# Matmuls of 274 columns, two of them shared between neighbours, in place of 272

## The chip, the core and the metric

The program runs on one core of one Trainium2 chip. TensorE (PE in the profile) multiplies, with its weight loads shown apart as PEld; VectorE (DVE), ScalarE (ACT) and GpSimd (POOL) work element by element, and SyncE (SP) issues most DMAs. The metric is the device time of one execution in microseconds. Three runs of the kernel before took 2904.58, 2910.63 and 2912.99 us, a median of 2910.63 us. The profile comes from one more execution, of 2907.33 us.

## The reference

One inference step of a decoder trunk of two layers, model width 1024, over 1024 new prompt tokens and 64 sample tokens (8 sequences of 8), in float32:

```python
# layer 0: short gated convolution, layer 1: differential attention
gb, gc, h = jnp.split(x @ w_in, 3, axis=-1)            # w_in: 1024 x 3072
...                                                    # u = gc * h, three taps over time
y = (gb * conv) @ w_out
xp = _layernorm(ALPHA * xp + mp, ln_mix_g[i], ln_mix_b[i])

def _swiglu(x, w_in, w_out):                           # w_in: 1024 x 5632, w_out: 2816 x 1024
    gate, up = jnp.split(x @ w_in, 2, axis=-1)
    return (jax.nn.silu(gate) * up) @ w_out
xp = _layernorm(ALPHA * xp + _swiglu(xp, w_ffn_in[i], w_ffn_out[i]), ln_ffn_g[i], ln_ffn_b[i])
```

The three products that matter here are `x @ w_in` of the convolution and of the two feed-forward blocks. Attention, with its cache of 2048 past positions for each sample sequence, lies between them and is not touched.

## The kernel before

**The input products.** Each of the three large products is done by a Strassen scheme with seven smaller products in place of eight. Tokens are cut into two halves of 544 columns (`HALF`), and inputs and outputs into halves of their features. For the inputs, seven combinations of the four blocks lie in SBUF, each split into a high and a low part of the type float32r (`Combos`, tiles `xh` and `xl`, of 128 partitions, 7 operands, 4 blocks of 128 features and 544 columns). Weights are combined and split in the same way on the way in (`Weights.make`: tiles `ws`, made by a copy on ACT, L76, and a subtraction on DVE, L77).

**One product.** `in_type` (L216) runs a list of work items. An item is seven products, numbered 1 to 7, in an order written out in `order`; a product is done by `mm` (L233). Since a bank of PSUM holds 512 float32 values and a half has 544 columns, `mm` takes the half in two chunks of `CW` = 272 columns, one in each of two banks. For each chunk it runs over 4 blocks of 128 features and over 3 passes (high times high, high times low, low times high): 12 matmuls for a chunk, 24 for a product, each with its own weight load and a moving operand of 128 partitions by 272 columns (L240). Convolution has 12 items, each feed-forward block 22, so there are 56 x 7 x 24 = 9408 such matmuls.

**What follows a product.** Products 1, 6, 5 and 3 of an item add up in one pair of banks (tile `pin1`), 7 and 4 in another, 2 in a third. After 1, 6 and 5 ACT copies the sum so far out of PSUM (L254); after 2, 5 and 4 DVE adds a sum to a copy (L258); after 3 the item's class ends it (`put.last`). Both read the two chunks in one instruction, as 2 runs of 272 columns.

**What sets the order.** On PE the order inside `in_type` is that of the code (`manual_schedule`). On ACT, DVE, POOL and SP a scheduler of the framework places the instructions; it estimates when each can start. Weights are made up to seven products ahead (`prep`).

**The other stages.** Output products (`out_type`, L321) use matmuls of 512 columns with three passes; the projections of attention (L930) use matmuls of 256 columns with the same three passes, between which single steps of the sample attention run.

Of the kernel before, what the change touches and what calls it, by code (L numbers as in the profile page):

```python
# [14 lines left out]
ALU = mybir.AluOpType  # L15
# [11 lines left out]
CH = ((0, 32), (32, 32), (64, 240), (304, 272), (576, 240), (816, 272))  # L27
HALF = NT // 2
CW = HALF // 2
TT = (0,) + tuple(NS + P * i for i in range(NP // P))  # L30
F = 2816
FT = F // P
# [16 lines left out]
def decoder_kernel(ctx: ExitStack, tc: tile.TileContext, i_: dict, o_: dict):  # L49
    nc = tc.nc  # L50
    PE, ACT, DVE, POOL, SP = nc.tensor, nc.scalar, nc.vector, nc.gpsimd, nc.sync
# [36 lines left out]
    def passes(ah, al, bh, bl):  # L88
        return ((ah, bh), (ah, bl), (al, bh))
# [126 lines left out]
    def in_type(psum, x, work):  # L216


        order = [(0, 1), (0, 2)]
        for n in range(len(work)):  # L220
            order += [(n, 7), (n, 6)] + ([(n + 1, 1)] if n + 1 < len(work) else []) + [(n, 5)]
            order += ([(n + 1, 2)] if n + 1 < len(work) else []) + [(n, 4), (n, 3)]
        made, nxt = {}, 0
        banks = {}

        def prep(upto):
            nonlocal nxt
            while nxt < min(upto, len(order)):
                n, p = order[nxt]
                made[n, p] = work[n][0].make(p)  # L230
                nxt += 1

        def mm(ps, w, p, start, chunks=(0, 1)):  # L233
            for c in chunks:
                cs = slice(c * CW, c * CW + CW)
                for k in range(4):
                    ks = slice(k * P, k * P + P)
                    b = OPERAND[p]
                    for m, (a, y) in enumerate(passes(w[:, 0, ks], w[:, 1, ks], x.h[:, b, k, cs], x.l[:, b, k, cs])):
                        PE.matmul(ps[:, c, :CW], a, y, start=(start and k == 0 and m == 0),  # L240
                                  stop=(k == 3 and m == 2), skip_group_check=True)

        prep(6)
        with tc.manual_schedule(engines={mybir.EngineType.PE}):
            for at, (n, p) in enumerate(order):
                put = work[n][1]
                w = made.pop((n, p))
                if p in (1, 2, 7):
                    banks[n, p] = psum.tile([P, 2, 512], F32, name=f"pin{p}", tag="b")
                ps = banks[n, {1: 1, 6: 1, 5: 1, 3: 1, 7: 7, 4: 7, 2: 2}[p]]  # L250
                mm(ps, w, p, p in (1, 2, 7))
                v = ps[:, :, :CW]
                if p in (1, 6, 5):
                    ACT.copy(put.dst({1: 0, 6: 2, 5: 3}[p]), v)  # L254
                if p in (2, 5, 4):
                    blk = {2: 0, 5: 3, 4: 2}[p]
                    d = put.dst(blk)
                    DVE.tensor_tensor(d, d, banks[n, 7][:, :, :CW] if p == 5 else v, op=ALU.add)  # L258
                    put.done(blk)
                elif p == 3:  # L260
                    put.last(v)
                prep(at + 7)
# [171 lines left out]
    def ffn_in(layer, psum, xc):  # L434
        with tc.tile_pool(name=f"fst{layer}", bufs=2, reuse_waits="tile") as stage:
            class Put:
                def __init__(self, f):
                    self.f, self.sg, self.hf = f, {}, None

                def gate(self, t):  # L440
                    if t not in self.sg:
                        self.sg[t] = stage.tile([P, 2, CW], F32, name=f"sg{t}", tag=f"sg{t}", bufs=2 - t)
                    return self.sg[t]

                def dst(self, blk):
                    if blk == 0:
                        return self.gate(0)
                    if self.hf is None:
                        self.hf = stage.tile([P, 2, 2, CW], F32, name="hf", tag="hf")
                    return self.hf[:, blk - 2]  # L450

                def done(self, blk):
                    if blk == 0:
                        ACT.activation(self.sg[0], self.sg[0], AF.Silu)
                    elif blk == 2:
                        DVE.tensor_tensor(self.hf[:, 0], self.hf[:, 0], self.sg[0], op=ALU.mult)

                def last(self, ps):
                    ACT.activation(self.gate(1), ps, AF.Silu)
                    DVE.tensor_tensor(self.hf[:, 1], self.hf[:, 1], self.sg[1], op=ALU.mult)  # L460
                    SP.dma_start(h_dram[layer][self.f], self.hf.rearrange("p a c n -> p (a c n)"))

            in_type(psum, xc, [(Weights(i_["wfi"][layer, 2 * f], i_["wfi"][layer, 2 * f + 1]), Put(f))
                               for f in range(FT)])
# [9 lines left out]
    with tc.tile_pool(name="psum0", bufs=4, space=PSUM) as psum:  # L474
        with tc.tile_pool(name="xc0", bufs=1, reuse_waits="tile") as xcp:
            xc = Combos(xcp)

            with tc.tile_pool(name="cvp", bufs=1, reuse_waits="tile") as cvp:
# [11 lines left out]
                for ch in range(2):  # L490
                    blk = {}
                    for t, k in ((0, 0), (0, 1), (1, 0), (1, 1)):
                        x = blk[k, t] = cv("u" if t else "gc")[:, 0:4 * CW].rearrange("p (k t) -> p k t", k=4)
                        at = 0
# [4 lines left out]
                    cs = slice(ch * CW, ch * CW + CW)  # L499
# [110 lines left out]
                for f0 in range(0, KT, 2):  # L610
                    gate = Gate(f0)
                    for m, put in ((1, gate), (2, Mix(f0, gate)), (0, Out(f0, gate))):
                        work.append((Weights(i_["wci"][3 * f0 + m], i_["wci"][3 * f0 + 3 + m]), put))
                in_type(psum, xc, work)
                POOL.dma_start(o_["conv_p"], cpT)
                POOL.dma_start(o_["conv_s"], csT)
# [16 lines left out]
    with tc.tile_pool(name="kvp", bufs=1, reuse_waits="tile") as kvp, \  # L633
# [276 lines left out]
        with tc.manual_schedule(engines={mybir.EngineType.PE}):  # L910
            for pr in range(4):
                for ty, dst in enumerate((q_dram, o_["k_p"], o_["v_p"])):
# [6 lines left out]
                    for tg in range(2):  # L919
                        nat = ap2.tile([P, 4, 256], F32, name="nat", tag="pr", bufs=4)  # L920
                        first = pr == ty == tg == 0
                        ps = [None] * 4
                        for kh, t in [(kh, t) for kh in range(2) for t in range(4)] if first else [(None, t) for t in range(4)]:
                            t0 = TT[1 + 4 * tg + t]
                            if t % 2 == 0 and not kh:
                                ps[t] = ps[t + 1] = ps2.tile([P, 2, 512], F32, name="psqkv", tag="s2")
                            for k in range(KT) if kh is None else range(4 * kh, 4 * kh + 4):
                                cs = slice((k % 4) * 256, (k % 4) * 256 + 256)
                                for n, (a, b_) in enumerate(passes(xTh, xTl, his[k // 4], los[k // 4])):
                                    PE.matmul(ps[t][:, t % 2, :256], a[:, k, t0:t0 + P], b_[:, cs],  # L930
                                              start=(k == 0 and n == 0), stop=(k == KT - 1 and n == 2),
# [85 lines left out]
        def mixed(h, i, r1, A, vn, ost):  # L1017
            aT = ap2.tile([P, KT, P], F32, name="aT", tag="aT", bufs=1)
            for g4 in range(0, i + 1, 4):
                m = min(4, i + 1 - g4)  # L1020
                ps = psb.tile([P, 4, P], F32, name="psaT", tag="pb")
                for k in range(m):
                    PE.transpose(ps[:, k, :], A[:, (g4 + k) * P:(g4 + k + 1) * P], ident)  # L1023
                (ACT.copy if g4 == 0 else DVE.tensor_copy)(aT[:, g4:g4 + m, :], ps[:, :m, :])
            return h, i, r1, aT, vn, ost
# [34 lines left out]
        for h in range(NH):  # L1060
# [4 lines left out]
            for n in range(8):  # L1065
# [4 lines left out]
                m = mixed(*todo.pop(0)) if len(todo) == 2 else None  # L1070
# [7 lines left out]
        for x in todo:  # L1078
            m = mixed(*x)
# [115 lines left out]
```

## Time and profile before

| | before |
|---|---|
| runs (us) | 2904.58, 2910.63, 2912.99 |
| profiled execution (us) | 2907.33, its span 2905.6 |
| mean granted TensorE clock | 0.971 |
| PE busy | 2728.5 us, 94% |
| DVE, ACT, POOL busy | 52%, 36%, 9% |
| DMA | 157 GB/s mean |

A matmul's record is longer than the distance to the next one, since matmuls are pipelined and their ends are modelled. The time that a stream of matmuls takes is therefore read from the starts of rows, not from their lengths. Where a row says x2, it stands for two matmuls after one another.

### The profile page before, as it was taken

How to read it: one execution, taken by the hardware profiler on the slowest of the kernel's cores; microseconds unless marked ns; L12 is line 12 of the kernel's file. 1: busy time of each engine (PE TensorE's matmuls, PEld its weight loads, DVE VectorE, ACT ScalarE, POOL GpSimd, SP SyncE). 2: the span in 40 equal slices, each digit the busy share in tenths (PEclk: the TensorE clock that was granted, in tenths of full speed). 3: DMA queues.
4: the chain of work that ended last, by engine and by line, in shares of the span. 5: the costliest groups of instructions: out<-in, count | busy, mean ns of one | idle time of the engine just before them, and what ended most of it. 6: DMA issues, size and time to landing. Idle time of an engine off the chain costs nothing.

```text
span 2905.6 us, 51121 instructions
## 1 busy us (share of the span) xinstructions
PE 2728.5 (94%) x20436; PEld 2364.7 (81%) x20436; DVE 1497.9 (52%) x2565; ACT 1043.0 (36%) x1921; POOL 253.4 (9%) x481
## 2 busy tenths in 40 slices
PE   6999879999998999899999999997889999989997
PEld 6999559999997677689888666665679999986676
DVE  7666476555552365522222666673775555532555
ACT  4222254333332244412122556562543333322343
POOL 0000010000000010111111232330100000000100
PEclk9999989999999999899999999998999999999999
DMA  3111652222223466775877888834622222234666
GB/s 123 67 60 62 199 182 81 75 82 72 79 73 118 139 212 202 228 260 200 278 275 254 287 299 309 288 110 144 211 77 80 73 82 75 75 100 147 203 190 191
DMA packets 187728, 454.95 MB, mean 157 GB/s; under 512 B 36545, under 2 KB 85330, under 8 KB 187490
## 3 DMA queue, kind: packets, MB, share of 16 engines
q1 hardware_dynamic: 175442, 408.88, 42.3%
q0 software_dynamic: 11904, 42.55, 4.3%
q8 instruction: 160, 2.62, 0.4%
q14 instruction: 78, 0.64, 0.1%
q10 hardware_dynamic: 144, 0.26, 0.0%
HBM read 387.44 MB, written 64.17 MB: 155 GB/s over the span
## 4 chain that ended last, share of the span: by engine, by line
PE 64%; issue 23%; DMA 5%; DVE 3%; ACT 2%; POOL 2%; SPq 1%; DVEq 0%; POOLq 0%; ACTq 0%
PE pin L240 25%; PE pout L321 14%; PE psqkv L930 10%; PE psS L995 3%; PE psO L833 3%; PE pso L1030 2%; PE psS L775 2%; PE psaT L1023 1%; PE pouts L324 1%; DMA raw<-wfo 1%; PE psq L717 1%; DMA hr<-h_dram 1%; DVE wlo L77 1%; PE psS L998 1%; DVE xl L77 0%
## 5 line engine op out<-in xcount | busy, mean ns | idle before, releaser
L240 PE MATMUL pin<-xh,ws 128*128 128x272 f32 x6272 | 1199.4, 290 | 39.6 <-ACT ws L76 18.6
L240 PEld LDWEIGHTS pin<-xh,ws 128*128 128x128 f32 x6272 | 1000.3, 190 | 43.4 <-ACT ws L76 19.1
L240 PE MATMUL pin<-xl,ws 128*128 128x272 f32 x3136 | 914.2, 292 | 2.2 <-DVE xl L77 2.1
L240 PEld LDWEIGHTS pin<-xl,ws 128*128 128x128 f32 x3136 | 594.6, 190 | 3.1 <-DVE xl L77 3.1
L321 PE MATMUL pout<-whi,hh 128*128 128x512 f32 x960 | 391.4, 409 | 56.6 <-ACT hh L76 43.6
L77 DVE TENSOR_TENSOR wlo<-raw,whi 128x1024 fp32r<-128x1024 f32 x204 | 250.8, 1230 | 291.0 <-ACT whi L76 260.7
L321 PE MATMUL pout<-whi,hl 128*128 128x512 f32 x960 | 381.5, 400 | 4.2 <-DVE hl L77 4.2
L321 PE MATMUL pout<-wlo,hh 128*128 128x512 f32 x960 | 381.2, 398 | 0.0
L76 ACT CAST whi<-raw 128x1024 fp32r<-128x1024 f32 x204 | 213.6, 1048 | 287.7 <-DMA raw<-wfo 145.6
L321 PEld LDWEIGHTS pout<-whi,hh 128*128 128x128 f32 x960 | 184.3, 192 | 145.9 <-ACT hh L76 69.2
L77 DVE TENSOR_TENSOR ws<-s,ws 128x512 fp32r<-128x512 f32 x224 | 154.5, 690 | 141.6 <-ACT ws L76 141.0
L930 PE MATMUL psqkv<-whi,xTh 128*128 128x256 f32 x768 | 222.6, 290 | 2.4 <-DVE xTl L77 2.4
L321 PEld LDWEIGHTS pout<-whi,hl 128*128 128x128 f32 x960 | 183.9, 192 | 49.5 <-DVE hl L77 8.0
L321 PEld LDWEIGHTS pout<-wlo,hh 128*128 128x128 f32 x960 | 184.5, 192 | 38.2 <-DVE wlo L77 0.3
L930 PE MATMUL psqkv<-wlo,xTh 128*128 128x256 f32 x768 | 214.7, 279 | 0.0
L930 PE MATMUL psqkv<-whi,xTl 128*128 128x256 f32 x768 | 214.4, 279 | 0.0
L76 ACT CAST ws<-s 128x512 fp32r<-128x512 f32 x224 | 138.8, 620 | 205.8 <-PE pin L240 103.8
L77 DVE TENSOR_TENSOR hl<-hr,hh 128x384 fp32r<-128x384 f32 (+1 forms) x180 | 94.4, 525 | 184.0 <-ACT hh L76 183.8
L76 ACT CAST hh<-hr 128x384 fp32r<-128x384 f32 (+1 forms) x180 | 85.4, 475 | 260.8 <-PE pout L321 167.1
L94 POOL TENSOR_SCALAR rs_t<-lss 128x1 f32<-128x1 f32 x32 | 22.0, 686 | 1691.9 <-ACT pout L355 1085.7
L77 DVE TENSOR_TENSOR ws<-raw,ws 128x512 fp32r<-128x512 f32 x168 | 115.4, 688 | 99.6 <-ACT ws L76 99.6
L930 PEld LDWEIGHTS psqkv<-whi,xTh 128*128 128x128 f32 x768 | 145.0, 189 | 18.0 <-issue 14.1
(219 smaller groups left out, 3269.7 us busy)
## 6 DMA issues: line engine op xcount, KB each, us to landing
raw<-wfo SPq DMA_DIRECT2D x132, 512.0 KB, 3.9
kpg<-ck SPq DMA_DIRECT2D x128, 512.0 KB, 5.3
vpg<-cv SPq DMA_DIRECT2D x128, 512.0 KB, 4.9
raw<-wfi SPq DMA_DIRECT2D x88, 512.0 KB, 3.3
h_dram<-hf SPq DMA_DIRECT2D x44, 544.0 KB, 2.7
raw<-wci SPq DMA_DIRECT2D x24, 512.0 KB, 3.3
raw<-wco SPq DMA_DIRECT2D x24, 512.0 KB, 3.8
x_dram<-x SPq DMA_DIRECT2D x24, 512.0 KB, 3.0
```

Of the source, the lines that this page charges most:

```text
L76: ACT.copy(hi, src)
L77: (eng or DVE).tensor_tensor(lo, src, fv(hi), op=ALU.subtract)
L240: PE.matmul(ps[:, c, :CW], a, y, start=(start and k == 0 and m == 0), stop=(k == 3 and m == 2), skip_group_check=True)
L321: PE.matmul(ps[:, hf, :], a, b, start=(f == 0 and m == 0), stop=(f == nf - 1 and m == 2))
L324: PE.matmul(pq[half * NS:half * NS + NS, 0, :], hs, raw[:, half * 512:half * 512 + 512], start=(f == 0), stop=(f == nf - 1), skip_group_ch ...
L717: PE.matmul(psq[half * NS:half * NS + NS, pr * 256:pr * 256 + 256], xsT[:, 4 * kh + k, :], raws[half][:, k, :], start=(kh == 0 and k == 0) ...
L775: PE.matmul(ps[32 * t:32 * t + 32, n, :], qp[:, 2 * t + h2, :], kp[:, 2 * t + h2, :], start=(h2 == 0), stop=(h2 == 1), skip_group_check=True)
L833: PE.matmul(O[32 * t:32 * t + 32, :], PT[:, p, 32 * t:32 * t + 32], vp[:, 2 * t:2 * t + 2, :].rearrange("p h d -> p (h d)"), start=(p == 0 ...
L930: PE.matmul(ps[t][:, t % 2, :256], a[:, k, t0:t0 + P], b_[:, cs], start=(k == 0 and n == 0), stop=(k == KT - 1 and n == 2), skip_group_che ...
L995: PE.matmul(svs[c][:, bk, :], a[cp, i, :], b_[cp, bk * w:bk * w + w], start=(m == 0), stop=(m == 2), skip_group_check=True)
L998: PE.matmul(svs[c][:, nb - 1, w - P:w], idb, cmask, start=False, stop=True, skip_group_check=True)
L1030: PE.matmul(po, aT[:, k, :], vn[:, k, :], start=(k == 0), stop=(k == i))
```

## The change

`mm` takes chunks of 274 columns. The first reads columns 0 to 273 of the half, the second columns 270 to 543, so that both read columns 270 to 273. The first chunk's results are put from column 2 of its bank and the second's from column 0, so that in both banks the 272 columns that belong to the chunk lie at 2 to 273. All readers take them from there.

```diff
+MW = CW + 2
...
             for c in chunks:
-                cs = slice(c * CW, c * CW + CW)
+                cs = slice(c * (CW - 2), c * (CW - 2) + MW)
+                at = 2 - 2 * c
                 for k in range(4):
...
-                        PE.matmul(ps[:, c, :CW], a, y, start=(start and k == 0 and m == 0),
+                        PE.matmul(ps[:, c, at:at + MW], a, y, start=(start and k == 0 and m == 0),
                                   stop=(k == 3 and m == 2), skip_group_check=True)
...
-                v = ps[:, :, :CW]
+                v = ps[:, :, 2:2 + CW]
...
-                    DVE.tensor_tensor(d, d, banks[n, 7][:, :, :CW] if p == 5 else v, op=ALU.add)
+                    DVE.tensor_tensor(d, d, banks[n, 7][:, :, 2:2 + CW] if p == 5 else v, op=ALU.add)
```

On PE no instruction changes its place; waits do. These are the first matmuls of the program's second product (bank pair `pin_303`), in the first stage, before the change and then after it:

```order
L240 MATMUL pin_303<-xh,ws 128x272 [waits Activation_49]
L240 MATMUL pin_303<-xl,ws 128x272
L240 MATMUL pin_303<-xh,ws 128x272 [waits DVE_49]
L240 MATMUL pin_303<-xh,ws 128x272
L240 MATMUL pin_303<-xl,ws 128x272
```

```order
L244 MATMUL pin_303<-xh,ws 128x274 [waits Activation_49]
L244 MATMUL pin_303<-xl,ws 128x274 [waits DVE_49]
L244 MATMUL pin_303<-xh,ws 128x274 [waits DVE_49]
L244 MATMUL pin_303<-xh,ws 128x274
L244 MATMUL pin_303<-xl,ws 128x274
```

The first chunk's matmuls now wait for the second chunk's inputs as well, of which they read two columns; the second chunk, 12 matmuls later, waited for them anyway.

On ACT and on DVE two neighbours change places in four places each: three in the convolution and one at the start of the first feed-forward block. This is the one on ACT in the feed-forward block, before and then after; `sg_4231` is the copy of a product's sum out of PSUM and `ws` a weight tile for a later product:

```order
L76 CAST ws<-s_4199 128x512
L76 CAST ws<-s_4234 128x512
L254 COPY sg_4231<-pin_4206 128x544
L76 CAST ws<-raw 128x512
L76 CAST ws<-s_4233 128x512
```

```order
L79 CAST ws<-s_4199 128x512
L79 CAST ws<-s_4234 128x512
L79 CAST ws<-raw 128x512
L258 COPY sg_4231<-pin_4206 128x544
L79 CAST ws<-s_4233 128x512
```

The copy out of PSUM has moved behind one cast of a weight tile. On POOL and SP nothing moves.

## Rows read from the trace of the kernel before

**Rows 1.** The page: busy time, share of the span and instructions.

```profile
PE 2728.5 (94%) x20436; PEld 2364.7 (81%) x20436; DVE 1497.9 (52%) x2565; ACT 1043.0 (36%) x1921; POOL 253.4 (9%) x481
```

**Rows 2.** The page: the chain that ended last, by line.

```profile
PE pin L240 25%; PE pout L321 14%; PE psqkv L930 10%; PE psS L995 3%; PE psO L833 3%; PE pso L1030 2%; PE psS L775 2%; PE psaT L1023 1%; PE pouts L324 1%; DMA raw<-wfo 1%; PE psq L717 1%; DMA hr<-h_dram 1%; DVE wlo L77 1%; PE psS L998 1%; DVE xl L77 0%
```

**Rows 3.** Stretches of the input products: length, busy time by engine, clock, DMA.

```profile
core 0: us, PE busy (x) PEld busy (x) DVE busy (x) ACT busy (x) POOL busy (x), PEclk, DMA share, GB/s
30.00:60.00 30.00, 26.30 (x193) 26.14 (x194) 26.77 (x43) 11.82 (x20) 0.20 (x2) 0.87 0.21 71
443.00:480.00 37.00, 33.68 (x246) 32.45 (x245) 28.45 (x44) 18.68 (x31) 0.00 (x0) 0.95 0.24 86
480.00:900.00 420.00, 420.00 (x3340) 420.00 (x3339) 212.70 (x314) 140.51 (x238) 0.00 (x0) 1.00 0.22 76
2129.00:2160.00 31.00, 28.49 (x201) 27.31 (x202) 25.66 (x40) 16.57 (x27) 0.00 (x0) 0.93 0.21 70
```

**Rows 4.** The page: groups of matmuls of the input products.

```profile
L240 PE MATMUL pin<-xh,ws 128*128 128x272 f32 x6272 | 1199.4, 290 | 39.6 <-ACT ws L76 18.6
L240 PE MATMUL pin<-xl,ws 128*128 128x272 f32 x3136 | 914.2, 292 | 2.2 <-DVE xl L77 2.1
```

**Rows 5.** Timeline of PE, 272 columns, steady (start, length, what).

```profile
600.05 0.29 PE L240 MATMUL pin<-xl,ws 128*128 128x272 f32 x1
600.17 0.41 PE L240 MATMUL pin<-xh,ws 128*128 128x272 f32 x2
...
602.82 0.41 PE L240 MATMUL pin<-xh,ws 128*128 128x272 f32 x2
603.07 0.29 PE L240 MATMUL pin<-xl,ws 128*128 128x272 f32 x1
```

**Rows 6.** Timeline of PE, 272 columns, early in the first stage.

```profile
33.70 0.82 PE L240 MATMUL pin<-xh,ws 128*128 128x272 f32 x2 [8.54 <-DVE ws L77]
34.33 0.43 PE L240 MATMUL pin<-xl,ws 128*128 128x272 f32 x1
...
37.05 0.43 PE L240 MATMUL pin<-xl,ws 128*128 128x272 f32 x1
```

**Rows 7.** Granted clock of the stretches of rows 5, 6, 8 and 9.

```profile
core 0: us, PE busy (x), PEclk, DMA share, GB/s
34.00:37.00 3.00, 3.00 (x14) 0.50 0.00 0
400.50:402.60 2.10, 2.10 (x11) 1.00 0.02 4
600.00:603.10 3.10, 3.10 (x27) 1.00 0.02 7
1385.00:1386.10 1.10, 1.10 (x12) 1.00 1.06 331
1404.80:1405.80 1.00, 1.00 (x11) 1.00 0.40 152
```

**Rows 8.** Timeline of PE, 256 columns (L930), in two places.

```profile
1385.01 0.28 PE L930 MATMUL psqkv<-whi,xTl 128*128 128x256 f32 x1
...
1386.07 0.28 PE L930 MATMUL psqkv<-whi,xTl 128*128 128x256 f32 x1
...
1404.78 0.28 PE L930 MATMUL psqkv<-whi,xTl 128*128 128x256 f32 x1
...
1405.80 0.28 PE L930 MATMUL psqkv<-whi,xTl 128*128 128x256 f32 x1
```

**Rows 9.** Timeline of PE, 512 columns (L321).

```profile
400.51 0.39 PE L321 MATMUL pout<-whi,hh 128*128 128x512 f32 x1
...
402.57 0.39 PE L321 MATMUL pout<-wlo,hh 128*128 128x512 f32 x1
```

**Rows 10.** Timeline of DVE ahead of the first stage's second product.

```profile
30.56 1.28 DVE L77 TENSOR_TENSOR xl<-u,xh 128x1088 fp32r<-128x1088 f32 x1
31.76 1.28 DVE L507 TENSOR_TENSOR u<-u,gc 128x1088 f32<-128x1088 f32 x1
32.96 0.68 DVE L77 TENSOR_TENSOR ws<-raw,ws 128x512 fp32r<-128x512 f32 x1
```

**Rows 11.** Waits: engine, line, waited for: us in total, times, longest.

```profile
ACT hf L254 <- PE pin L240: 186.4, 88, 4.4
```

## Prediction

> **What bounds the kernel now.** I read the page's busy times first. PE is busy for 94% of the span, DVE for 52%, ACT for 36% [rows 1]. The chain that ended last puts its largest share, 25%, on the line that the change touches [rows 2]. Then I cut the input products into stretches. In the steady one, 480 to 900 us, PE is busy for all of 420 us at a granted clock of 1.00, while DVE works 212.7 us, ACT 140.5 us and the DMA engines 22% [rows 3]. So there the stream of matmuls alone sets the time, and what one matmul costs there is paid 1:1. In the first microseconds of each of the three input stages it is otherwise: DVE works 26.8 of 30, 28.5 of 37 and 25.7 of 31 us, PE has gaps, and the three stretches hold 193 + 246 + 201 = 640 matmuls [rows 3]. There are 6272 + 3136 = 9408 matmuls of this line [rows 4], so about 8770 run where PE sets the pace.
>
> What one costs is read from starts. From 600.05 to 603.07 us there are 24 matmuls: 3.02 us, 125.8 ns each [rows 5], at the full clock of 2.4 GHz [rows 7]. At the half clock, 1.2 GHz [rows 7], 12 of them take 34.33 to 37.05 us, 226.7 ns each [rows 6]. That is 272 / 1.2: one column a cycle and nothing else. At the full clock the columns account for 272 / 2.4 = 113.3 ns, and 12.5 ns are left over. This extra is the whole question, because the columns themselves are worth little.
>
> The extra is not one number. Matmuls of 256 columns on another line, at the full clock too, come at 9 in 1385.01 to 1386.07 us, 117.8 ns, in one place, and at 9 in 1404.78 to 1405.80 us, 113.3 ns, 20 us later in the same loop [rows 7, 8]. With 256 / 2.4 = 106.7 ns taken off, the extra is 11.1 ns there and 6.7 ns here, for the same shape, the same three passes, and the same operand tiles by name. Matmuls of 512 columns take 400.51 to 402.57 us for 9, 228.9 ns: an extra of 15.6 ns [rows 7, 9]. So at the full clock a stream falls into one of several steady rhythms, and the width alone doesn't say into which.
>
> **The change part by part.** *Two more columns.* 2 / 2.4 = 0.83 ns for each matmul. Over 8770 that is +7.3 us, if the extra stays.
>
> *The extra.* No row shows 274 columns, a chunk whose first column isn't a multiple of 16, or results that start at column 2 of a bank, so the extra is bounded from both sides. The nearest rows are 6.7 ns (256 columns, the quick rhythm) and 15.6 ns (512 columns). The far ends are no extra at all, as at the half clock, and one group of 16 columns more (below, under the rivals). I take 6.7 ns. The reason is a choice between the two: going from the slow rhythm of 256 to 512, the extra rises by 4.5 ns over 256 columns, so a straight line gives 11.4 ns at 272, and the measured 12.5 ns lies 1.1 ns above it. The present width thus stands in the slow rhythm, at the high side of it, and never leaves it in a stretch of 3340 matmuls [rows 3]. Every start of a new matmul moves by two columns against the weight loads and the results of the one before, which is the kind of thing that must differ between the two rhythms at 256. With 6.7 ns, a matmul costs 274 / 2.4 + 6.7 = 120.8 ns, 5.0 ns less than 125.8. Over 8770 this is -43.9 us, the two columns included. The other ends: no extra, 114.2 ns, -11.7 ns each, -102 us; 15.6 ns, 129.8 ns each, +3.9 ns, +35 us.
>
> The Trainium skill ("TensorE: Matmul & The Clock Gate", Back-to-back issue gap) states that a warm matmul is spaced at columns / 2.4 plus a fixed 2.5 ns. By that, 272 columns would take 115.8 ns and 274 would take 116.7 ns. Its fixed part disagrees with this trace, which has 6.7 to 15.6 ns [rows 5, 8, 9]; its form, a fixed part that doesn't depend on a column or two, is the first rival below.
>
> *The wait of the first chunk.* It now waits for the second chunk's inputs. That can cost at most the 12 matmuls of a chunk that would have run earlier, 12 x 0.2267 = 2.7 us, in the first product where it bites; it can gain nothing. In the second product of the program PE waits until 33.70 us for a weight tile, whose subtraction starts at 32.96 us, behind two DVE instructions that come after those of this product's inputs [rows 6, 10]. The inputs are there first, so I take 0. Behind the waiting matmul only its own product is queued. In the feed-forward blocks the two extra columns belong to a piece of 128 tokens that the first chunk reads anyway.
>
> *The swaps on ACT and DVE.* In four places a copy out of PSUM goes one weight cast of about 0.6 us later. What hides it: before these copies ACT sits idle for PE, 186.4 us in 88 times, 2.1 us each [rows 11], and PE works on another pair of banks for a whole product, 3.0 us, before it returns. Without this cover it would be 4 x 0.6 = 2.4 us. I take 0.
>
> *What is late next.* At 120.8 ns a matmul, the 420 us stretch would take 403 us, and DVE's 212.7 us in it would be 53%, ACT's 140.5 us 35%, DMA 23%. Nothing else becomes the bound, so the gain arrives whole.
>
> The sum: 2907.33 us, the profiled execution's own time, -43.9 = 2863.4 us. The median of the runs lies 3.3 us above that execution, so I say 2865 us.
>
> **Rivals.** *The extra stays at 12.5 ns.* Only the columns count: +7.3 us, 2914.6 us by the profiled execution. For it: the extra of 256 to 512 columns moves by a few ns only, and two columns are a small step. Against it: the two rhythms at one and the same width.
>
> *The stream falls into a slower rhythm.* With the 15.6 ns of the widest matmuls the time is 2907.3 + 35 = 2942 us. Its place is each matmul of the input products, its price 3.9 ns a matmul, and it decides from an extra of 12.7 ns on, where the loss passes 0.3%. For it: the extra grows with the width in the slow rhythm. Against it: two columns are a small part of the 240 that lead to 512.
>
> *The cut starts cost.* Before, all chunks start at a multiple of 16 columns and are 17 times 16 columns long; after, the second starts at 270, and each touches 18 groups of 16. If reads go by such groups, each matmul pays up to 16 columns, 6.7 ns at 2.4 GHz, 58 us in all, 2966 us; if they go by groups of 4 columns, 69 groups in place of 68, 1.67 ns, +14.6 us, 2922 us. For it speaks nothing in the rows but that no width off a multiple of 16 occurs; against it, that the half clock shows no cost beyond columns [rows 6]. The Trainium skill ("SBUF — State Buffer", A bandwidth-pool intuition that's wrong) states that SBUF has lines of 16 bytes, four float32 values, that each new line costs something, and that two hits in a line are enough for the full rate; a chunk that begins in mid-line has two. By it the smaller price would be the most. No row here shows a start inside a line.
>
> **How the numbers follow.** An effect below 0.3%, 8.7 us, can't be told from no change. A lower extra than 10.7 ns makes the kernel faster by more than that (0.99 ns x 8770 matmuls). Between the ends 6.7 and 15.6 ns that is 45% of the way; because the present rhythm is high for its width, I give the forecast case 0.55. The unchanged extra, +0.25%, gets 0.18, all of it within 0.3%. The slower rhythm gets 0.17 and the cut starts 0.10, both slower by over 0.3%. The likeliest case alone ranges from an extra of 1 ns, 2814 us, to 10.7 ns, 2899 us. To hold 8 in 10 the range must take in the unchanged extra, the smaller price of the cut starts and the milder half of the slower rhythm: 2815 to 2938 us.
>
> **What would show it.** In the profile after, the matmuls of 274 columns in the steady stretch must come 24 in 2.90 us where they came 24 in 3.02 us, with PE still busy throughout and the starts of the other lines' matmuls unchanged. 24 in 3.04 us is the unchanged extra; 3.12 us the slower rhythm; 3.06 or 3.18 us the cut starts. The first chunk's wait is right if the second product still starts within a microsecond of 33.7 us. I'd be wrong in kind if the distance of the matmuls fell and the time didn't: then something other than PE bounds the steady stretch, against [rows 3].

## The result, and the profile after

The change makes the kernel slower by 0.4%. Nine runs of each on the same chips gave a median of 2921.89 us (2920.61 to 2928.86) after and 2911.43 us (2903.08 to 2918.27) before; the ratio is 1.004, with a 95% interval from 1.0026 to 1.0054. The profiled execution took 2920.61 us, 13.3 us more than that of before. The time lies in the range forecast, on the other side of no change.

The page of the kernel after, its two groups of matmuls of the input products, answers to [rows 4]:

```profile
L244 PE MATMUL pin<-xh,ws 128*128 128x274 f32 x6272 | 1212.0, 292 | 38.5 <-ACT ws L79 18.5
L244 PE MATMUL pin<-xl,ws 128*128 128x274 f32 x3136 | 916.3, 292 | 2.9 <-DVE xl L80 2.8
```

The idle time before them is what it was, 38.5 + 2.9 us against 39.6 + 2.2 [rows 4]. The steady stretch, same columns as [rows 3]:

```profile
480.00:900.00 420.00, 420.00 (x3304) 420.00 (x3303) 210.57 (x312) 138.22 (x236) 0.00 (x0) 1.00 0.22 78
```

PE is busy throughout at the full clock, and gets through 3304 matmuls where it got through 3340. So the loss in this stretch is all in the distance between matmuls. PE's timeline after, as in [rows 5]:

```profile
599.85 0.29 PE L244 MATMUL pin<-xl,ws 128*128 128x274 f32 x1
599.98 0.42 PE L244 MATMUL pin<-xh,ws 128*128 128x274 f32 x2
...
602.90 0.29 PE L244 MATMUL pin<-xl,ws 128*128 128x274 f32 x1
```

These are 24 matmuls in 3.05 us; taken from the starts of all 24-matmul blocks of the three stages, the median is 3.053 us, against 3.020 before. That is 127.2 ns a matmul in place of 125.8. With 274 / 2.4 = 114.2 ns for the columns, the extra is 13.0 ns, not the 6.7 that I took. Over the 8770 matmuls at PE's pace, 1.38 ns make 12.1 us, within the 7.6 to 15.7 us of the interval. Elsewhere the rhythms are those of before: the 256-column matmuls of the attention projections, which I leaned on, still run at 113.3 and 117.8 ns.

The second product's start in the first stage, behind the new wait, against [rows 6]:

```profile
34.00 0.59 PE L244 MATMUL pin<-xh,ws 128*128 128x274 f32 x1 [7.01 <-DVE ws L80]
```

It starts 0.3 us later, released by the same weight tile.

### The profile page after: what moved, and what is told of

Its sections match the earlier page's. It is cut to its first block, busy times and chain, and to the rows that moved or that the text cites. A ratio compares the mean times of both kernels' runs of the same rounds, so it can differ in the third digit from the quotient of the medians.

```text
span 2918.8 us, 51121 instructions
## 1 busy us (share of the span) xinstructions
PE 2741.1 (94%) x20436; PEld 2377.6 (81%) x20436; DVE 1498.7 (51%) x2565; ACT 1044.4 (36%) x1921; POOL 259.2 (9%) x481
## 4 chain that ended last, share of the span: by engine, by line
PE 65%; issue 23%; DMA 4%; DVE 4%; ACT 2%; POOL 1%; SPq 0%; DVEq 0%; POOLq 0%; ACTq 0%
PE pin L244 25%; PE pout L325 15%; PE psqkv L934 10%; PE psS L999 3%; PE psO L837 3%; PE pso L1034 2%; PE psS L779 2%; PE psaT L1027 1%; PE pouts L328 1%; DMA hr<-h_dram 1%; PE psq L721 1%; DVE wlo L80 1%; DMA raw<-wfo 1%; DVE xl L80 1%; PE psS L1002 1%
## 5 line engine op out<-in xcount | busy, mean ns | idle before, releaser
L244 PE MATMUL pin<-xh,ws 128*128 128x274 f32 x6272 | 1212.0, 292 | 38.5 <-ACT ws L79 18.5
L244 PE MATMUL pin<-xl,ws 128*128 128x274 f32 x3136 | 916.3, 292 | 2.9 <-DVE xl L80 2.8
L80 DVE TENSOR_TENSOR ws<-raw,ws 128x512 fp32r<-128x512 f32 x168 | 115.5, 689 | 101.1 <-ACT ws L79 101.1
```

What stands on the lines that cost most here:

```text
L80: (eng or DVE).tensor_tensor(lo, src, fv(hi), op=ALU.subtract)
L244: PE.matmul(ps[:, c, at:at + MW], a, y, start=(start and k == 0 and m == 0), stop=(k == 3 and m == 2), skip_group_check=True)
```

## Experiments

My theory now: the two added columns cost their 0.83 ns, and the extra depends on where the moving columns start, not on how many there are. Rivals: the extra depends on the width; on where results lie in the bank; on neighbours that add into the same bank; on the weight load beside each matmul; on how the stream is entered. The measure is the time of 24 matmuls (one product), from its first start to the first start of the next, as the median over all products; where lines are shown, they are two starts 24 matmuls apart. In the kernel before 365 of the 392 products take 3.020 us, and the median is the same in all three stages, so one profile is enough for it. Where a run has no single value the text says so. Each run's time stands beside that of the kernel before on the same chip. Most are of single executions, and 17 of the kernel before on one chip ranged from 2898.34 to 2916.53 us, so a few us between two such times say nothing.

**Results moved in the bank, columns as before (e1).**

```diff
-PE.matmul(ps[:, c, :CW], a, y, ...
+PE.matmul(ps[:, c, 2:2 + CW], a, y, ...        # and all readers from 2
```

> Chunks of 272 columns as before (starts 0 and 272), but results lie from column 2 of both banks and are read from there. Width theory (the extra per matmul depends on the number of columns alone): 24 steady matmuls in 3.020 us as before. Result theory (the shifted start in the bank costs): 24 in about 3.04 us or more, the part of the rise from 3.020 to 3.053 beyond the two columns. Start theory (the second chunk's shifted first column costs): 3.020 us.

Measured 3.020 us; program 2903.67 us against 2902.49. At 272 columns the place of the results costs nothing.

**The second chunk's start moved, 272 columns (e2).**

```diff
-cs = slice(c * CW, c * CW + CW)
+cs = slice(c * 270, c * 270 + 272)
```

> Chunks of 272 columns, results from column 0, but the second chunk reads columns 270 to 541 in place of 272 to 543, so its results belong to other columns than the reference's. Start theory: the second chunk's 12 matmuls get slower, 24 in about 3.03 us or more, and the two chunks' halves differ. Width theory and result theory: 3.020 us.

Measured 3.020 us; 2906.37 against 2902.49. The halves do differ (125.0 and 126.8 ns on average, against 125.4 and 126.2), but the sum doesn't. At 272 columns the cut start is free, against the start theory in its simple form.

**274 columns with whole starts (e3).**

```diff
-cs = slice(c * CW, c * CW + CW)
+cs = slice(c * 256, c * 256 + 274)
```

> Chunks of 274 columns with results from column 0 and both first columns multiples of 16 (0 and 256); the second chunk computes other columns than the reference's. Width theory: 24 in 3.053 us, all of the change's rise. If the columns alone count and the rest of the rise is start or result: 24 x (125.83 + 0.83) = 3.040 us.

The timeline of PE, 24 matmuls apart:

```profile
599.95 0.29 PE L240 MATMUL pin<-xl,ws 128*128 128x274 f32 x1
...
602.99 0.29 PE L240 MATMUL pin<-xl,ws 128*128 128x274 f32 x1
```

3.04 us, 126.7 ns: the extra is 12.5 ns, exactly that of 272 columns. So two more columns leave the extra as it was. This is the run on which the failed step of the forecast falls: going from 272 to 274 columns doesn't move the rhythm. Program 2912.15 against 2902.49.

**The other 0.013 us: start or results (e5, e6).** Both have 274 columns; e5 has the change's starts with results at column 0, e6 whole starts with the change's results.

```diff
+cs = slice(c * 270, c * 270 + 274)              # e5, results at 0 and 0
+cs = slice(c * 256, c * 256 + 274)              # e6, results at 2 and 0
```

> Chunks of 274 columns that start at 0 and 270 as in the change, but results from column 0 in both banks, so that what is read of the first chunk is right and of the second is moved by two columns. The change has 24 matmuls in 3.053 us and 274 columns with whole starts have 3.040. If the last 0.013 us come from the start at 270 (start theory): 3.053 us. If from results that lie at column 2 in one bank and 0 in the other (result theory): 3.040 us.

> Chunks of 274 columns that start at 0 and 256, results from column 2 of the first bank and column 0 of the second as in the change; the second chunk computes other columns than the reference's. Start theory: 24 in 3.040 us. Result theory: 3.053 us.

PE's timeline of e5, then of e6:

```profile
599.94 0.29 PE L240 MATMUL pin<-xl,ws 128*128 128x274 f32 x1
...
602.99 0.29 PE L240 MATMUL pin<-xl,ws 128*128 128x274 f32 x1
```

```profile
599.90 0.29 PE L240 MATMUL pin<-xl,ws 128*128 128x274 f32 x1
...
602.94 0.29 PE L240 MATMUL pin<-xl,ws 128*128 128x274 f32 x1
```

3.053 and 3.040 us by the median (2918.08 and 2910.66 us against 2904.54). The rest of the rise, 0.55 ns a matmul, comes with the start at 270. It isn't the second chunk's alone: both chunks average 126.7 ns in e3 and 127.2 ns after the change, so the start of one moves the rhythm of both.

**Four more columns in each chunk (e11).** 276 columns, starts 0 and 268. The title and the expectations call shared what each chunk has over 272; the two chunks of the change have four columns in common, 270 to 273, and those of e11 have eight.

```diff
-MW = CW + 2                                     # starts 0 and 270
+MW = CW + 4                                     # starts 0 and 268
```

> The change with four shared columns in place of two: chunks of 276 columns, starts 0 and 268, results from column 4 of the first bank and 0 of the second. 268 is a multiple of 4 columns but not of 16; 270 was a multiple of 2. If only a start inside a group of 4 columns costs: extra 12.5 ns, 24 in 24 x (115 + 12.5) = 3.060 us. If any start off a multiple of 16 costs, as at 270: 3.073 us.

```profile
600.00 0.28 PE L240 MATMUL pin<-xl,ws 128*128 128x276 f32 x1
...
603.03 0.29 PE L240 MATMUL pin<-xl,ws 128*128 128x276 f32 x1
```

Products took 3.031 to 3.035 us, 3.035 by the median, neither of the two expected: 126.5 ns for 276 columns, less than the 127.2 of the change's 274, an extra of 11.5 ns. Program 2908.56 us against 2907.02. The extra isn't a price for starts off some multiple; it goes up and down with the layout.

**Other widths (e7, e8).** 256 columns at the starts of before, and 288 with 16 shared columns.

```diff
+n = CW if first else 256                        # e7, starts c * 272
+cs = slice(c * 256, c * 256 + 288)              # e8
```

> The same loop with matmuls of 256 columns (but for the first into a cleared bank, which keeps 272); the last 16 columns of each chunk are left out. If the extra is fixed for this loop, 12.5 ns whatever the width: 24 in 24 x (106.67 + 12.5) = 2.860 us. If the width alone decides as on the line of 256 columns: 24 in 2.826 us in the slow rhythm or 2.720 us in the quick one, with both seen in one run.

> The same loop with chunks of 288 columns, starts 0 and 256, results from column 16 of the first bank and 0 of the second: the change with 16 shared columns in place of 2, every start a multiple of 16. Fixed extra: 24 in 24 x (120 + 12.5) = 3.180 us. Extra on the line from 256 in the slow rhythm to 512: 24 x (120 + 11.7) = 3.160 us. A fall into the quick rhythm of 6.7 ns: 3.040 us.

PE's timeline of e7:

```profile
600.07 0.28 PE L243 MATMUL pin<-xl,ws 128*128 128x256 f32 x1
...
602.91 0.28 PE L243 MATMUL pin<-xl,ws 128*128 128x256 f32 x1
```

e7 took 2.840 us, between the two slower values expected: 118.3 ns (117.5 in the first chunk, 119.2 in the second), near the slow rhythm and never the quick one. e8 took 3.173 us, 132.2 ns, an extra of 12.2; 2963.08 us against 2904.54. In the runs so far, widths from 256 to 288 in this loop all have an extra of 11 to 13 ns.

**Neighbours in different banks (e4).**

```diff
-for c in chunks: for k in range(4): for m in range(3):
+for k in range(4): for m in range(3): for c in chunks:
```

> 272 columns, starts 0 and 272 as before, but the two chunks alternate: each weight block and pass is used for the first chunk and then for the second, so neighbouring matmuls add into different banks. Bank theory (the extra comes from adding into the bank that the matmul before still writes): the extra falls from 12.5 ns toward the 6.7 ns of the quick rhythm, 24 in about 2.88 us, the program some 45 us faster. Width theory: 24 in 3.020 us, no change in time but for the first products.

3.027 us where the bank theory had 2.88; program 2906.68 against 2902.49. The bank theory falls.

**Half the weight load (e9).**

```diff
-PE.matmul(ps[:, c, :CW], a, y, ...
+PE.matmul(ps[:64, c, :CW], a[:, 0:64], y, ...   # but for the first into a cleared bank
```

> 272 columns as before, but all matmuls other than the first into a cleared bank load 64 columns of weights in place of 128 and give 64 rows of results; the other 64 rows are left out. Load theory (the extra comes from the weight load that runs beside each matmul): with half the load the extra falls by about half, 24 in 24 x (113.33 + 6.2) = 2.870 us. If the extra belongs to the stream of moving columns or to the switch between matmuls: 3.020 us.

```profile
599.78 0.29 PE L243 MATMUL pin<-xl,ws 128*64 128x272 f32 x1
...
602.77 0.29 PE L243 MATMUL pin<-xl,ws 128*64 128x272 f32 x1
```

2.987 us: the extra falls from 12.5 to 11.1 ns, not to 6.2. The load has a small share at most; this run also halves the rows of results, and which of the two gave the 1.4 ns isn't shown.

**The place of the columns (e12, e13, e16).** All three keep the loop and take other columns of the same operand. Where before all starts are multiples of 272 columns (1088 bytes) from the operand's first, they are now multiples of 256 columns (1024 bytes), with 256 and with 272 columns to a matmul, and of 288 columns (1152 bytes) with 256.

```diff
-cs = slice(c * CW, c * CW + n)                  # within block k, of 544 columns
+cs = slice((2 * k + c) * 256, (2 * k + c) * 256 + n)        # e12: n = 256, e13: n = 272
+cs = slice((2 * k + c) % 7 * 288, (2 * k + c) % 7 * 288 + 256)   # e16
```

> 256 columns as in the run of that width, but every chunk starts at a multiple of 256 columns of its operand, as the moving operands of the attention projections do; other columns than the reference's are computed. If the place of the columns decides the rhythm: 24 in 24 x 113.3 = 2.720 us. If not: 2.826 us, as without it.

> 272 columns from starts that are multiples of 256 columns; other columns than the reference's are computed. If the place decides: an extra near 6.7 ns, 24 in 2.880 us. If not: 3.020 us give or take the 0.03 that other layouts showed.

> 256 columns from starts that are multiples of 288 columns (1152 bytes) in place of 256; other columns than the reference's are computed. If a start at a multiple of 128 bytes is enough for the quick rhythm: 24 in 2.720 us. If it takes starts at multiples of 1024 bytes, or of 256: about 2.83 us.

PE's timelines of e12, e13 and e16, each 24 matmuls:

```profile
599.77 0.28 PE L244 MATMUL pin<-xl,ws 128*128 128x256 f32 x1
...
602.49 0.28 PE L244 MATMUL pin<-xl,ws 128*128 128x256 f32 x1
```

```profile
600.02 0.29 PE L244 MATMUL pin<-xl,ws 128*128 128x272 f32 x1
...
602.98 0.29 PE L244 MATMUL pin<-xl,ws 128*128 128x272 f32 x1
```

```profile
599.92 0.28 PE L245 MATMUL pin<-xl,ws 128*128 128x256 f32 x1
...
602.75 0.28 PE L245 MATMUL pin<-xl,ws 128*128 128x256 f32 x1
```

2.72 us, 113.3 ns, for e12: the quick rhythm, extra 6.7 ns, which e7 with the same width in the same loop never had. This holds for products 3, 4, 5 and 6. Products 1, 2 and 7, whose chunks begin with one matmul of 272 columns, take 2.787 us: six distances of 116 to 123 ns, then 113.3. 2.96 us, 123.3 ns, for e13: the extra of 272 columns falls from 12.5 to 10.0 ns, not to the 6.7 expected, and the program takes 2874.90 us against 2900.59. 2.83 us, 117.8 ns, for e16: steps of 1152 bytes keep the slow rhythm.

So the place of the moving columns matters, and of the steps tried only 1024 bytes gave the quick rhythm. They allow it and don't ensure it: the attention projections read at such steps too and run in both rhythms [rows 8]. What counts is the step inside an operand, and not that a start is a multiple of 1024 bytes in the tile: operands lie 8704 bytes, 8.5 times 1024, apart, and in e12 products on even ones (3 and 4) and on odd ones (5 and 6) all take 2.720 us.

**Entering the stream anew (e14).**

```diff
+for q in range(4):                              # after each chunk of 12
+    PE.matmul(ps[32 * q:32 * q + 32, c, 288:416], <32 columns of w>, <128 columns of x>, ...
```

> The kernel before with four narrow matmuls (32 columns of weights, 128 moving columns, results into unused columns of the bank) after each chunk of 12, so that the stream is broken off and entered anew 784 times, as the attention projections are by the sample attention. If the entry decides the rhythm and 272 columns have a quick one too: some chunks run their 12 matmuls at about 120 ns and others at 125.8. If 272 columns know only one rhythm: all chunks at 125 to 126.5 ns, and the program is longer by what the narrow matmuls take.

The trace shows eight narrow matmuls after each chunk for the four of the code. From their second matmul on, the 784 chunks run at 124.8 to 126.8 ns (1st to 95th percentile): breaking the stream off brought no quick rhythm at these starts. The program took 3332.61 us against 2900.59.

**Uneven chunks, and uneven chunks laid out apart (e10, e15).** Both compute everything. e10 cuts the half at column 256; e15 also stores each operand as 4 blocks of 256 columns and then 4 of 288, so that the first chunk's matmuls start at multiples of 1024 bytes.

```diff
-for c in chunks:                                # e10
-    cs = slice(c * CW, c * CW + CW)
+for c, x0, n in ((0, 0, 256), (1, 256, 288)):
+    cs = slice(x0, x0 + n)                      # readers: one instruction for each bank
...
-self.h = pool.tile([P, 7, 4, HALF], ...)        # e15 as well
+self.h = pool.tile([P, 7, 4 * HALF], ...)       # chunk c: columns 1024 * c on, 4 x (256 or 288)
```

> All is computed; the half is cut into chunks of 256 and 288 columns, without shared ones, and every reader of a product takes the two banks in two instructions, some 0.2 us more each on ACT or DVE. From the widths tried: 117.8 ns for 256 and 132.2 for 288 give 125.0 on average against 125.8, 24 in 3.000 us, -7 us or -0.25% in all, if ACT and DVE hide the added instructions. If each width keeps a fixed extra of 12.5 ns: 3.020 us and no change. If the added instructions or the uneven banks come onto the path: slower than before, with PE idle in the steady stretch.

> All is computed. The operands lie by chunk: 4 blocks of 256 columns after one another, then 4 blocks of 288, so that the first chunk's matmuls start at multiples of 1024 bytes and the second's at multiples of 1152; every reader takes the two banks in two instructions. Place theory: the first chunk runs at 113.3 ns; the second at 126.7 ns if multiples of 128 bytes are enough (24 in 2.88 us, -50 us), at 132 ns if not (24 in 2.944 us, -28 us or -1%). If the place had only worked together with the other columns computed in that run: 24 in 2.993 us as with 256 and 288 before, -8 us.

e10: 2.993 us for 24 matmuls, 117.4 ns in the first chunk and 132.0 in the second. 2898.60 us against 2907.02, ratio 0.9971 (0.9960 to 0.9983): -8.4 us where -7 was expected, with PE busy for 419.2 of the 420 us of the steady stretch.

e15: 2886.04 us against 2905.76, ratio 0.9937 (0.9921 to 0.9954). PE's timeline, two products after one another:

```profile
599.83 0.28 PE L254 MATMUL pin<-xl,ws 128*128 128x256 f32 x1
...
600.85 0.28 PE L254 MATMUL pin<-xl,ws 128*128 128x256 f32 x1
601.20 0.30 PE L254 MATMUL pin<-xl,ws 128*128 128x288 f32 x1
...
602.39 0.30 PE L254 MATMUL pin<-xl,ws 128*128 128x288 f32 x1
602.77 0.28 PE L254 MATMUL pin<-xl,ws 128*128 128x256 f32 x1
...
603.84 0.28 PE L254 MATMUL pin<-xl,ws 128*128 128x256 f32 x1
```

The first chunk, of 256 columns, runs 9 of its matmuls in 1.02 us in the one product, 113.3 ns, and in 1.07 us in the next. In an unbroken stream the two rhythms alternate strictly, one product quick and the next slow, whichever of the seven it is, 115.5 ns on average; products take 2.944 and 3.009 us in turn. Near the end of each stage PE breaks off between products 6 and 5, with 1.06 us from start to start; there both have the same rhythm, quick in two stages and slow in one, so it isn't tied to the product or its weights. The 288 columns stay at 132.5 ns. So the expected -28 us came to -19.7 (about -16 by the rows; the interval is -13 to -23): the quick rhythm came in every other product only. e15 beats the kernel before by 0.6%.

## Why the prediction was wrong

- **What bounds the kernel** was right: PE was busy for all 420 us of the steady stretch in both kernels, and each ns between matmuls was paid.
- **The two columns**, 0.83 ns a matmul and +7.3 us, were right: 3.040 against 3.020 us for 24 matmuls (e3).
- **The extra** is the step that failed: "I take 6.7 ns", because every start moves by two columns against the loads. It came to 13.0 ns, and the -43.9 us to +12.1 by the rows. Two things stood behind the step. One was that the width decides which rhythm a stream falls into; e3 and e6 show an unchanged 12.5 ns at 274. The other was that the two rhythms of [rows 8] say something of this loop. They belong to a line whose moving operand is a weight tile read at multiples of 256 columns (in the code `(k % 4) * 256`), 1024 bytes; the input products read theirs at multiples of 272 columns, or 1088 bytes. e12 against e7 shows that this difference lets a stream of 256 columns be quick; 272 columns at the same steps still had 10.0 ns (e13). The change left the steps alone, but for the second chunk's start, moved from 272 to 270. The number was a fair reading of the trace, of another layout.
- **The straight line** from 256 to 512 columns, by which 272 stood 1.1 ns too high, had no meaning: 272, 274, 276 and 288 gave 12.5, 12.5 or 13.0, 11.5 and 12.2 ns by layout.
- **The rivals.** The unchanged extra (2914.6 us) described the greater part: 7.3 of the 12.1 us worked out from the rows. The Trainium skill ("TensorE: Matmul & The Clock Gate", Back-to-back issue gap), which the prediction quotes beside it, gives its 2.5 ns as the gap of an isolated matmul; no run here has one, and the streams here have 6.7 to 15.6 ns. The rest, 0.55 ns and 4.8 us, comes with the cut start (given 0.10). That rival's smaller price, 1.67 ns or 14.6 us with the two columns counted in, came nearest of all to the measured 1.38 ns and 12.1 us, its 2922 us to the measured 2921.89. But that is luck: it isn't the granule of 4 columns that I described, since the start at 270 cost nothing with 272 columns, and chunks of 276 from 268 were quicker than 274 from 270. The Trainium skill ("SBUF — State Buffer", Door 1: The DMA port swizzle; the prediction names another section) has lines of 16 bytes and a penalty for each new one. If the tiles begin on a line, the chunks of the change, of e3 and of e11 all touch 69 lines, and they took 127.2, 126.7 and 126.5 ns: the count of lines alone doesn't set the time. The slower rhythm of 15.6 ns didn't come.
- **The first chunk's wait and the swaps** were rightly put at nothing: 0.3 us at the second product's start and no idle time on PE in the steady stretch.
- **The chances.** 0.55 for a fall of the extra rested on the ends of a range taken from two other lines, as if every value between were as likely. The input products themselves had shown one rhythm, 3.020 us in 365 of 392 products.

Open is what the extra is. It doesn't come from the results' place, the banks, or mainly the weight load. It depends on the steps between the starts of the moving columns; at steps of 1024 bytes also on the width (6.7 ns at 256 columns, 10.0 at 272) and on what ran just before (e12, e15). Why 274 columns from 270 have 0.55 ns more than the 12.5 of before, and 276 from 268 have 1.0 ns less, wasn't found.

## What to carry to other kernels

A rhythm seen on one line may be carried to another only if the operands are laid out alike: compare the steps between the starts of what is read, in bytes, before the width. Where matmuls follow one another without a gap, try laying the moving operand out so that the starts are multiples of 1024 bytes from its first column, before changing how many columns a matmul has. At 272 columns that was worth 2.5 ns of 125.8, in a run that computes other columns (e13); in one that computes everything (e15) it came for one chunk of two, in every other product. Take columns added to a stream that sets the time at what they cost by themselves, until a run shows otherwise.

## What was not expected of the hardware

- Matmuls of 272 columns went from 125.8 to 123.3 ns (e13), and those of 256 from 118.3 (e7) to 113.3 (e12), by the place of the columns alone.
- Two rhythms can alternate from product to product for a whole stage, 2.944 and 3.009 us in turn (e15).
- In the kernel before nearly every product takes 3.020 us, while single distances within its 24 matmuls range from 120 to 132 ns and repeat. Not every layout is so regular: products of e11 take 3.031 to 3.035 us.
- Half the weight load, with half the rows of results, took 1.4 ns off 125.8 (e9).
